# A hybrid decoder layer on one core: pinning the products of the DeltaNet systems' recursion behind the last evicted projection

## The chip, the cores and the metric

The kernel runs on one core of a Trainium2 chip. The core has a matrix engine, TensorE (PE in the rows; its weight loads are PEld), and three engines for the rest: VectorE (DVE), ScalarE (ACT) and GpSimd (POOL). SyncE (SP) issues the DMAs. Each engine works through its own list of instructions, and semaphores tie the lists together. The metric is the device time of one execution in microseconds (us), the median of several runs; the profile is of one further execution.

## The reference

One decoder layer over 1040 tokens (16 learned ones, then 1024), 1024 channels, all in float32: half a SwiGLU feed-forward block, a mixer, a second half block, a norm. The mixer holds two branches of 8 heads of 128: gated DeltaNet and retention. The DeltaNet branch is where the change lies. Cut to it:

```python
def gdn_chunk_scan(q, k, v, g, beta, state, chunk):
    ...
    a = jnp.where(strict, jnp.einsum("bhncd,bhnmd->bhncm", k_beta, k) * decay, 0.0) + jnp.eye(chunk, dtype=q.dtype)
    solve = functools.partial(lax.linalg.triangular_solve, left_side=True, lower=True)
    u = solve(a, v * beta[..., None])
    w = solve(a, k_beta * jnp.exp(g)[..., None])
    ...
    def step(s, xs):
        qk_c, u_c, w_c, qd_c, kd_c, gl_c = xs
        v_new = u_c - jnp.einsum("bhck,bhkv->bhcv", w_c, s)
        o = jnp.einsum("bhck,bhkv->bhcv", qd_c, s) + jnp.einsum("bhcm,bhmv->bhcv", qk_c, v_new)
        s = s * jnp.exp(gl_c)[..., None, None] + jnp.einsum("bhck,bhcv->bhkv", kd_c, v_new)
        return s, o
```

For each head and each chunk of tokens a unit lower triangular system `a` is solved, and then a scan carries a 128x128 state from chunk to chunk.

## The kernel before, in words

Every float32 matmul of the projections is made of three passes (L158 to L160) over numbers split in a high and a low part: ACT makes the high part of a weight tile (`wh`, L136), POOL or DVE the low part (`wl`, L137). The weights come in tiles `wraw` by DMA. The projections of the mixer are made in pairs by seven products of half blocks instead of eight (`project`), for which DVE forms sums and differences of raw weight tiles (L708, L709, L711, L712). A product ends in a bank of PSUM with the tag `mm`, of which there are two; it is evicted by a copy on ACT (L667, L705, L715, L717) or by an addition on DVE (`add`, L649). The next product but one needs the bank again.

The DeltaNet mixer is woven from four generators that each give a step at a time. `bulk` is the filling work: for each head the projection of keys and values (`kv`), a pair of gate projections, the projection of queries and of the output gate. Three others lead beside it, each at a rate of its own in steps per filling step: `all_scans` 0.6, `all_systems` 0.95, `all_queries` 0.53. `idle(n)` lets n steps of a generator pass with nothing in them. The program so traced is then put in order, engine by engine, when it is built: the builder keeps the dependencies and follows its own estimate of when each operand is there. `tc.issue_after(x)` adds one more condition to the instructions of its block: those on x's engine stand behind x in that engine's list.

`gdn_systems` prepares one head: silu and a short convolution of the keys (`cb`, L1021, L1023, L1026), the products of the keys with themselves (L1122), scaled into `X` (L1126); their 16x16 diagonal blocks (`x16`, L1131, L1132) are written to HBM and read back, repeated for each row of a block, as `xr` (two DMAs, L1144), because the recursion that inverts the blocks needs them so. The recursion is 15 times a product (`pr`, L1160) and an update of `u` by it (L1161), all on DVE, strictly one after the other; all 15 products read `xr`. Behind it PE takes `u` (L1171), and a chain of small matmuls (L1180 to L1240) between DVE and ACT turns the 16x16 inverses into the 128x128 inverse `Ut`. `gdn_scan` of a head then carries the state: in each chunk PE makes two products that read the state (L1300, L1302), two copies on ACT follow (`vn`, L1304, L1305), PE makes the update (L1308), and DVE adds it (`st`, L1310), for which the next chunk waits. Scan steps of one head lie beside the system of the next.

The pool `raw` holds the projections that are convolved or become gates, three buffers of 128x1043; `Ut` has one buffer.

Of the kernel before, what the change touches and what calls it, by code (L numbers as in the profile page):

```python
# [10 lines left out]
F32 = mybir.dt.float32  # L11
F32R = mybir.dt.float32r
AF = mybir.ActivationFunctionType
ALU = mybir.AluOpType
PSUM = bass.MemoryType.PSUM

P = 128
# [11 lines left out]
NCH = SEQ // P  # L29
CK = NCH + 1  # L30
# [27 lines left out]
W_REC = 2  # L58
W_OUT = 3
W_DMA = 1  # L60
STEPS = 1
FAST = [[(2,), (2,)], [(2,), (2,)]]
PLAIN = [[[['mm', 'mm'], ['px', 'px']], [['gx', 'gx'], ['mm', 'px']]], [[['gx', 'gx'], ['gx', 'px']], [['mm', 'gx'], ['mm', 'px']]]]
# [33 lines left out]
def hybrid_layer(ctx, tc, a):  # L97
    nc = tc.nc
    V, S, G, PE, SP = nc.vector, nc.scalar, nc.gpsimd, nc.tensor, nc.sync
# [11 lines left out]
    def psum(kind):  # L111
        return pp.tile([P, 512], F32, name=f"ps_{part[0]}_{kind}", tag=kind, bufs=PS_BUFS[kind])
# [162 lines left out]
    def ffn(fp, hidp, hT, hn, slots, spare, second, w_in, w_out, last_blocks, last_weights, tail, first, w0=None):  # L275
# [139 lines left out]
        def output(f, e, xs, steps):  # L415
# [13 lines left out]
            for i, (wh, wl) in weights():  # L429
                chain = i in (1, 3, 5)  # L430
                for j, (d, g0) in enumerate((d, g0) for d in range(2) for g0 in range(0, 2, gn)):
                    if i in (0, 1, 3):
# [8 lines left out]
                                           op0=ALU.mult, op1=ALU.add)  # L441
                for _ in range(STEPS):
                    next(steps, None)
# [62 lines left out]
    ps = psum("px")  # L506
# [132 lines left out]
    m_ctx = ExitStack()  # L639
# [5 lines left out]

    H1, H2 = slice(0, HM), slice(HM, 2 * HM)

    def add(out, x, ps):
        V.tensor_tensor(out=out, in0=x, in1=ps, op=ALU.add)  # L649

    def product(w, i, ps=None, last=True, grow=False):
        first = ps is None
# [93 lines left out]
    def idle(n):  # L746
        for _ in range(n):
            yield
# [10 lines left out]
    def run(steps):  # L759
        while True:  # L760
            try:
                next(steps)
            except StopIteration as e:
                return e.value
# [24 lines left out]
    ps = psum("gx")  # L789
# [65 lines left out]
    def chunk0(c):  # L855
        return (0, NM) if c == 0 else (NM + (c - 1) * P, P)
# [137 lines left out]
        ret_scan(h, *row)  # L994
    r_ctx.close()

    wide = m_ctx.enter_context(tc.tile_pool(name="raw", bufs=3, side="right", reuse_waits="tile"))
    mp = m_ctx.enter_context(tc.tile_pool(name="mix", bufs=1, side="right", reuse_waits="tile"))
    bp = m_ctx.enter_context(tc.tile_pool(name="systems", bufs=2, side="right", reuse_waits="tile"))
    sp = m_ctx.enter_context(tc.tile_pool(name="scan", bufs=2, side="right", reuse_waits="tile"))  # L1000
# [11 lines left out]
    def silu2(raw, which, col):  # L1012
        t0 = 0 if which else NM
        o = query_tile() if which < 2 else raw
        ct = col // P
        for b0, bn in MIX3:
            s0 = max(b0, t0)
            n = b0 + bn - s0
            d = slice(s0, s0 + n)
            c = cblk(n, wide)  # L1020
            S.activation(c, raw[:, s0:s0 + n], AF.Copy, scale=cw[:, ct:ct + 1])  # L1021
            for k in range(1, TAPS):
                V.scalar_tensor_tensor(out=c, in0=raw[:, s0 + k:s0 + k + n], scalar=cw[:, 24 * k + ct:24 * k + ct + 1],  # L1023
                                       in1=c, op0=ALU.mult, op1=ALU.add)
            yield
            S.activation(o[:, d], c, AF.Silu)  # L1026
            yield
        return o
# [66 lines left out]
    def gdn_systems(h, kraw, vraw):  # L1095
# [19 lines left out]
        ps = psum("px")  # L1115
        yield PE.matmul(ps[:NM, 0:NM], lhsT=kf[:, 0:NM], rhs=kf[:, 0:NM], start=True, stop=True)
        V.scalar_tensor_tensor(out=x16[:NM, NCH], in0=ps[:NM, 0:NM], scalar=nr2b[:NM, 0:1], in1=emm[:NM, h], op0=ALU.mult, op1=ALU.mult)
        for j in range(0, NCH, 2):
            ps = psum("px")
            for i in range(2):  # L1120
                c0, n = chunk0(j + i + 1)
                ins = PE.matmul(ps[:, i * P:(i + 1) * P], lhsT=kf[:, c0:c0 + P], rhs=kf[:, c0:c0 + P], start=True, stop=True)  # L1122
            yield ins
            for i in range(2):
                c = j + i
                V.scalar_tensor_tensor(out=X[:, c], in0=ps[:, i * P:(i + 1) * P], scalar=nr2b[:, c + 1:c + 2],  # L1126
                                       in1=ems[c // 4][:, c % 4], op0=ALU.mult, op1=ALU.mult)
# [14 lines left out]
        for t, d, o in ((xr1, x_d, 0), (xr2, x2_d, hb)):  # L1142
            src = d.rearrange("(b j) c i -> b j (c i)", j=BS)[:, o:o + hb].rearrange("b j x -> b (j x)")
            SP.dma_start(t.rearrange("p j c i -> p (j c i)"), src.unsqueeze(1).broadcast_to([P // BS, BS, src.shape[1]]))  # L1144
        yield from idle(W_DMA)
        vf = yield from silu2(vraw, 2, 2048 + h * DK)
        kvm = bp.tile([P, 2, P], F32, name="kvm", tag="Ac", bufs=1)
        ps = psum("px")
# [5 lines left out]
        u = bp.tile([P, CK, BS], F32, name="u", tag="u16", bufs=2)  # L1154
        V.tensor_copy(u, delta.unsqueeze(1).broadcast_to([P, CK, BS]))
        pr = bp.tile([P, CK, BS], F32, name="pr", tag="pr", bufs=1)
        for j in range(BS - 1):
            n = BS - 1 - j
            xj = xr1[:, j, :, j + 1:] if j < hb else xr2[:, j - hb, :, j + 1 - hb:]
            V.tensor_tensor(out=pr[:, :, :n], in0=xj, in1=u[:, :, j:j + 1].broadcast_to([P, CK, n]), op=ALU.mult)  # L1160
            V.tensor_tensor(out=u[:, :, j + 1:], in0=u[:, :, j + 1:], in1=pr[:, :, :n], op=ALU.add)  # L1161
            if j % 3 == 2:
                yield from idle(W_REC)
# [3 lines left out]
                        in1=par.unsqueeze(1).unsqueeze(3).broadcast_to([P, NCH, 2, BS]), op=ALU.mult)  # L1167
        Tc = bp.tile([P, NCH, B2], F32, name="Tc", tag="Tc", bufs=1)
        V.transpose(out=Tc, in_=Uc)
        ps = psum("px")  # L1170
# [4 lines left out]
        def blocks32(lhs, rhs):  # L1175
            ps = psum("px")
            for c in range(NCH):
                for q in range(4):
                    qs = slice(B2 * q, B2 * q + B2)
                    ins = PE.matmul(ps[qs, B2 * c:B2 * c + B2], lhsT=lhs[qs, c], rhs=rhs[qs, c], start=True, stop=True,  # L1180
                                    tile_position=(B2 * q, B2 * q))
            return ps[:, :NCH * B2].rearrange("p (c x) -> p c x", x=B2), ins

        ps, ins = blocks32(xoff, Tc)
# [3 lines left out]
        ps = psum("px")  # L1188
# [3 lines left out]
        ps, ins = blocks32(Ac, Uc)  # L1192
# [1 line left out]
        V.tensor_tensor(out=Uc, in0=Uc, in1=ps, op=ALU.add)  # L1194
        Tc = bp.tile([P, NCH, B2], F32, name="Tc", tag="Tc", bufs=1)
        V.transpose(out=Tc, in_=Uc)
        Ut = bp.tile([P, NCH, P], F32, name="Ut", tag="Ut", bufs=1)
        G.memset(Ut, 0.0)
        tmp = bp.tile([P, CK * BS * BS * 3 // 4], F32, name="tmp", tag="xr", bufs=1)
        for q in range(4):  # L1200
# [4 lines left out]
        ps = psum("px")  # L1205
# [9 lines left out]
        ps = psum("px")  # L1215
# [11 lines left out]
        ps = psum("px")  # L1227
# [4 lines left out]
        ps = psum("px")  # L1232
# [5 lines left out]
        ps = psum("px")  # L1238
# [113 lines left out]
    def branch(w, ys, b0, bn):  # L1352
        ps = psum("mm")[:, :bn]
        for j in range(0, KC, 2):
            mm3(ps, [(*w[k], ys[k][0][:, b0:b0 + bn], ys[k][1][:, b0:b0 + bn]) for k in (j, j + 1)], j == 0, j == KC - 2)
            yield BR
        return ps
# [53 lines left out]
    def all_systems():  # L1411
        while 0 not in kv:
            yield
        yield from idle(N0)
        for h in range(H):
            systems[h] = (query[h], *(yield from named(f"g{h}sys", when(kv, h, lambda *x: gdn_systems(h, *x)))))
# [28 lines left out]
    for j in range(KC):  # L1445
        w = load_w(cols(a["w_branch_gdn"], j * P))
        gt_j = yrow(gates_d[O_GA][j])
        for b0, bn in R2:
            s = slice(b0, b0 + bn)
            ps = run(branch(w, ya, b0, bn))  # L1450
# [11 lines left out]
    for b0, bn in _cut([0, 512, 768, SEQ]):  # L1462
        part[0] = "branch"
        for j in range(KC):
            w = load_w(cols(a["w_out"], j * P), eng=V if j % 2 else G)
            ps = run(branch(w, ms, b0, bn))
# [85 lines left out]
```

## Time and profile before

| what | value |
|---|---|
| median of 3 runs (lowest, highest) | 3054.97 us (3052.35, 3057.59) |
| the profiled execution: its own time, its span | 3054.29 us, 3052.6 us |
| PE busy over the span | 2905.5 us (95%) |
| DVE, ACT, POOL busy over the span | 1806.9, 1333.5, 1651.6 us |
| mean granted clock of TensorE | 0.977 of full speed |

The span runs from the first to the last instruction. The granted clock is the share of TensorE's full clock that it was given; it has two levels, 1.2 and 2.4 GHz, and 0.5 in a row is the lower one. The DeltaNet mixer runs from about 1240 to 2100 us of the span, a head in some 100 us. Idle time of an engine is put down, in the rows below, to the semaphore that ended it.

### The profile page before, as it was taken

To read this page: it belongs to the slowest core of one execution; us is meant where nothing else is said; L and a number is where in the kernel's file an instruction comes from. 1 tells how busy PE (TensorE), PEld (TensorE's weight loads), DVE (VectorE), ACT (ScalarE), POOL (GpSimd) and SP (SyncE) were. 2 spreads that over 40 slices of the span, in tenths; PEclk is the share of its full clock that TensorE was granted. 3 is DMA by queue.
4 is the path that set the end of the run, shared out by engine and by line. 5 is a ranking of instruction groups with operands and counts; after the bars stand their busy time and mean duration, and the time that the engine had idled before them with its cause. 6 is when DMAs were issued, how large, how long until landed. Compare 5 with 4: busy or idle time off the path is not lost. (4 is left out here: it accounts for less than half of the span.)

```text
span 3052.6 us, 55749 instructions
## 1 busy us (share of the span) xinstructions
PE 2905.5 (95%) x21463; PEld 2754.0 (90%) x21463; DVE 1806.9 (59%) x3299; ACT 1333.5 (44%) x2797; POOL 1651.6 (54%) x1419
## 2 busy tenths in 40 slices
PE   7999998999899999989999999999998999999998
PEld 6999998999898999978998899888888999998777
DVE  8455658777755445565555554562438655557765
ACT  4333334433545544444554555463224433335332
POOL 5555556654577655543555444445526655557652
PEclk8999999999999999989999999999999999999999
DMA  3455458633221221212212221244533355457642
GB/s 104 136 171 167 157 174 274 193 95 109 59 61 52 64 66 39 73 42 66 74 53 64 63 74 49 72 149 123 187 110 115 115 161 163 160 168 251 211 125 94
DMA packets 364413, 357.19 MB, mean 117 GB/s; under 512 B 29921, under 2 KB 294370, under 8 KB 361586
## 3 DMA queue, kind: packets, MB, share of 16 engines
q1 hardware_dynamic: 364080, 353.61, 37.2%
q8 instruction: 168, 2.75, 0.4%
q14 instruction: 99, 0.81, 0.1%
q10 hardware_dynamic: 66, 0.02, 0.0%
HBM read 263.24 MB, written 90.32 MB: 116 GB/s over the span
## 5 line engine op out<-in xcount | busy, mean ns | idle before, releaser
L137 POOL TENSOR_TENSOR wl<-wraw,wh 128x512 fp32r<-128x512 f32 x806 | 1098.8, 1371 | 1043.0 <-ACT wh L136 968.8
L136 ACT CAST wh<-wraw 128x512 fp32r<-128x512 f32 x864 | 535.9, 623 | 987.6 <-issue 229.3
L223 DVE TENSOR_TENSOR wraw<-wraw 128x512 f32<-128x512 f32 x42 | 51.5, 1226 | 163.7 <-DMA wraw<-ffn_w_in 157.1
L1023 DVE SCALAR_TENSOR_TENSOR cb<-raw,cw,cb 128x344 f32<-128x344 f32 (+2 forms) x216 | 130.7, 637 | 25.7 <-ACT cb L1021 24.0
L158 PE MATMUL ps_gate_mm<-act,wh 128*128 128x344 f32 (+1 forms) x352 | 122.6, 349 | 5.8 <-DVE raw L649 3.8
L158 PE MATMUL ps_start_mm<-on,wh 128*128 128x260 f32 x392 | 111.5, 284 | 3.1 <-ACT q L339 1.6
L159 PE MATMUL ps_gate_mm<-act,wh 128*128 128x344 f32 (+1 forms) x352 | 114.3, 325 | 0.0
L160 PE MATMUL ps_gate_mm<-act,wl 128*128 128x344 f32 (+1 forms) x352 | 114.3, 325 | 0.0
L158 PE MATMUL ps_ffn_mm<-on,wh 128*128 128x256 f32 (+1 forms) x376 | 109.5, 291 | 2.0 <-ACT q L339 1.6
L160 PE MATMUL ps_start_mm<-on,wl 128*128 128x260 f32 x392 | 110.8, 283 | 0.2 <-POOL wl L137 0.2
L159 PE MATMUL ps_start_mm<-on,wh 128*128 128x260 f32 x392 | 110.9, 283 | 0.0
L160 PE MATMUL ps_ffn_mm<-on,wl 128*128 128x256 f32 (+1 forms) x376 | 109.3, 291 | 0.0
L159 PE MATMUL ps_ffn_mm<-on,wh 128*128 128x256 f32 (+1 forms) x376 | 109.2, 290 | 0.0
L158 PE MATMUL ps_start_px<-on,wh 128*128 128x260 f32 x308 | 87.4, 284 | 1.9 <-DVE sg L295 1.9
L298 DVE TENSOR_TENSOR q<-q,q 128x260 f32<-128x260 f32 (+1 forms) x84 | 69.7, 829 | 31.8 <-ACT q L339 31.8
L160 PE MATMUL ps_start_px<-on,wl 128*128 128x260 f32 x308 | 87.7, 285 | 0.0
L159 PE MATMUL ps_start_px<-on,wh 128*128 128x260 f32 x308 | 87.6, 285 | 0.0
L159 PE MATMUL ps_start_mm<-ox,wh 128*128 128x260 f32 x292 | 83.4, 286 | 3.6 <-DVE ox L137 3.6
L158 PE MATMUL ps_start_mm<-ox,wh 128*128 128x260 f32 x292 | 83.8, 288 | 1.9 <-ACT ox L136 1.5
L160 PE MATMUL ps_start_mm<-ox,wl 128*128 128x260 f32 x292 | 83.7, 287 | 1.1 <-POOL wl L137 1.1
L388 DVE TENSOR_TENSOR sums<-sums 128x512 f32<-128x512 f32 x80 | 83.8, 1067 | 0.7
L158 PE MATMUL ps_ffn_px<-on,wh 128*128 128x256 f32 (+1 forms) x284 | 83.3, 293 | 0.9 <-ACT wh L136 0.9
(1654 smaller groups left out, 10913.1 us busy)
## 6 DMA issues: line engine op xcount, KB each, us to landing
wraw<-ffn_w_in SPq DMA_DIRECT2D x176, 256.0 KB
wraw<-w_in SPq DMA_DIRECT2D x168, 256.0 KB
sums<-ffn_w_out SPq DMA_DIRECT2D x80, 256.0 KB
sums_d<-sums SPq DMA_DIRECT2D x20, 1024.0 KB
wraw<-sums_d SPq DMA_DIRECT2D x80, 256.0 KB
opnd<-opnd_d SPq DMA_DIRECT2D x35, 520.0 KB
opnd<-opnd_d SPq DMA_DIRECT2D x35, 512.0 KB
wraw<-ffn_w_out SPq DMA_DIRECT2D x68, 256.0 KB
```

What stands on the lines that cost most here:

```text
L136: S.copy(hi, raw)
L137: (eng or G).tensor_tensor(out=lo, in0=raw, in1=hi.bitcast(F32), op=ALU.subtract)
L158: PE.matmul(ps, lhsT=wh, rhs=xh, start=first and i == 0, stop=False, skip_group_check=grow)
L159: PE.matmul(ps, lhsT=wh, rhs=xl, start=False, stop=False, skip_group_check=grow)
L160: PE.matmul(ps, lhsT=wl, rhs=xh, start=False, stop=last and i == n - 1, skip_group_check=grow)
L223: V.tensor_tensor(out=ru[0], in0=ru[0], in1=ru[1], op=ALU.add)
L298: V.tensor_tensor(out=x[:, grp], in0=x[:, grp], in1=g[:, grp], op=ALU.mult)
L388: tc.keep_in_program_order(V.tensor_tensor(out=out, in0=x, in1=y, op=op))
L1023: V.scalar_tensor_tensor(out=c, in0=raw[:, s0 + k:s0 + k + n], scalar=cw[:, 24 * k + ct:24 * k + ct + 1], in1=c, op0=ALU.mult, op1=ALU.add)
```

## The change

Three edits. First, each product `pr` of the recursion is traced inside `tc.issue_after(added[0])`, where `added[0]` is the DVE addition that `add` traced last: the product may not stand ahead of that addition on DVE. Second, six empty steps (`W_XR`) are put ahead of the recursion in each head's system. Third, the pool `raw` gets a fourth buffer and `Ut` a second.

```diff
@@ constants
+W_XR = 6
@@ mixer
+    added = [None]
+
     def add(out, x, ps):
-        V.tensor_tensor(out=out, in0=x, in1=ps, op=ALU.add)
+        added[0] = V.tensor_tensor(out=out, in0=x, in1=ps, op=ALU.add).ins
...
-    wide = m_ctx.enter_context(tc.tile_pool(name="raw", bufs=3, side="right", reuse_waits="tile"))
+    wide = m_ctx.enter_context(tc.tile_pool(name="raw", bufs=4, side="right", reuse_waits="tile"))
@@ gdn_systems
         pr = bp.tile([P, CK, BS], F32, name="pr", tag="pr", bufs=1)
+        yield from idle(W_XR)
         for j in range(BS - 1):
             n = BS - 1 - j
             xj = xr1[:, j, :, j + 1:] if j < hb else xr2[:, j - hb, :, j + 1 - hb:]
-            V.tensor_tensor(out=pr[:, :, :n], in0=xj, in1=u[:, :, j:j + 1].broadcast_to([P, CK, n]), op=ALU.mult)
+            with tc.issue_after(added[0]):
+                V.tensor_tensor(out=pr[:, :, :n], in0=xj, in1=u[:, :, j:j + 1].broadcast_to([P, CK, n]), op=ALU.mult)
             V.tensor_tensor(out=u[:, :, j + 1:], in0=u[:, :, j + 1:], in1=pr[:, :, :n], op=ALU.add)
             if j % 3 == 2:
                 yield from idle(W_REC)
...
-        Ut = bp.tile([P, NCH, P], F32, name="Ut", tag="Ut", bufs=1)
+        Ut = bp.tile([P, NCH, P], F32, name="Ut", tag="Ut", bufs=2)
```

In the changed program the lines of `gdn_systems` up to the recursion have numbers higher by 3, those behind the product by 5: the product is L1165, the update L1166, the scan's `st` L1315, the addition of a projection L652, the matmul that takes `u` L1176.

The order of instructions moves from the first head's convolutions to the end of the DeltaNet mixer; ahead of it and behind it the lists are the same. DVE's list around the first product of head 6, before (a row is line, operation, out<-in, shape of the output; `st` belongs to the scan of head 5, `raw` to an evicted gate projection):

```order
L1132 SCALAR_TENSOR_TENSOR x_21220<-Xc,masks,x_21220 128x128
L649 TENSOR_TENSOR raw<-raw,ps_gate_mm 128x344
L1317 TENSOR_TENSOR vt<-ps_g5scan_rx,vt 128x512
L649 TENSOR_TENSOR raw<-raw,ps_gate_mm 128x344
L1160 TENSOR_TENSOR pr<-xr,u 128x9x15
L1161 TENSOR_TENSOR u<-u,pr 128x9x15
L1310 SCALAR_TENSOR_TENSOR st<-st,elast,ps_g5scan_gx 128x128
L1160 TENSOR_TENSOR pr<-xr,u 128x9x14
```

The same place now:

```order
L652 TENSOR_TENSOR raw<-raw,ps_gate_mm 128x344
L711 TENSOR_TENSOR wraw<-wraw 128x512
L712 TENSOR_TENSOR wraw<-wraw 128x512
L714 TENSOR_TENSOR wraw<-wraw 128x512
L1315 SCALAR_TENSOR_TENSOR st<-st,elast,ps_g5scan_gx 128x128
L715 TENSOR_TENSOR wraw<-wraw 128x512
L652 TENSOR_TENSOR raw<-raw,ps_g6proj_mm 128x344
L1165 TENSOR_TENSOR pr<-xr,u 128x9x15
L1166 TENSOR_TENSOR u<-u,pr 128x9x15
L1165 TENSOR_TENSOR pr<-xr,u 128x9x14
```

Four weight sums, one addition to the scan's state and one more evicted projection now stand ahead of the first product. In heads 1, 2 and 5, too, the first product moves behind the addition of the projection that comes next.

DVE's list at the first product of head 4, before (`st` belongs to the scan of head 3):

```order
L1310 SCALAR_TENSOR_TENSOR st<-st,elast,ps_g3scan_gx 128x128
L649 TENSOR_TENSOR raw<-raw,ps_gate_mm 128x344
L1317 TENSOR_TENSOR vt<-ps_g3scan_rx,vt 128x512
L1160 TENSOR_TENSOR pr<-xr,u 128x9x15
L1161 TENSOR_TENSOR u<-u,pr 128x9x15
L649 TENSOR_TENSOR raw<-raw,ps_gate_mm 128x344
L1160 TENSOR_TENSOR pr<-xr,u 128x9x14
L1310 SCALAR_TENSOR_TENSOR st<-st,elast,ps_g3scan_gx 128x128
```

And now:

```order
L652 TENSOR_TENSOR raw<-raw,ps_gate_mm 128x344 x2
L1315 SCALAR_TENSOR_TENSOR st<-st,elast,ps_g3scan_gx 128x128
L1322 TENSOR_TENSOR vt<-ps_g3scan_rx,vt 128x512
L711 TENSOR_TENSOR wraw<-wraw 128x512
L1165 TENSOR_TENSOR pr<-xr,u 128x9x15
L712 TENSOR_TENSOR wraw<-wraw 128x512
L1166 TENSOR_TENSOR u<-u,pr 128x9x15
L714 TENSOR_TENSOR wraw<-wraw 128x512
L1165 TENSOR_TENSOR pr<-xr,u 128x9x14
L1166 TENSOR_TENSOR u<-u,pr 128x9x14
```

Here the first product moves behind the second of the two gate additions, but not behind the next projection; the next `st` stands eight rows behind it. Heads 3 and 7 are alike, and in head 0 the product moves behind one addition that stood three rows behind it.

## Rows read from the trace of the kernel before

**Rows 1.** PE's waits, 1240 to 2120 us: waiter <- releaser: total, times, longest

```profile
PE ps_g0sys_px L1171 <- DVE u L1161: 7.0, 1, 7.0
PE ps_g5scan_gx L1300 <- DVE st L1310: 5.6, 1, 5.6
PE ps_g1proj_mm L158 <- ACT zs L667: 4.2, 1, 4.2
PE ps_gate_mm L158 <- DVE raw L649: 3.8, 1, 3.8
PE ps_g2scan_gx L1300 <- DVE st L1310: 3.3, 2, 2.2
PE ps_g6scan_gx L1300 <- DVE st L1310: 2.3, 2, 2.0
PE ps_g4scan_gx L1300 <- DVE st L1310: 2.2, 1, 2.2
...
PE ps_g1proj_mm L158 <- DVE raw L649: 1.6, 1, 1.6
PE ps_g1scan_gx L1300 <- DVE st L1310: 1.5, 1, 1.5
PE ps_g2proj_mm L158 <- ACT raw L667: 1.3, 1, 1.3
```

**Rows 2.** DVE's waits over the same stretch

```profile
DVE pr L1160 <- DMA xr<-x_d: 37.7, 8, 7.7
```

**Rows 3.** Timeline of DVE, head 6: start, duration, instruction, idle time before it

```profile
1904.30 0.51 DVE L649 TENSOR_TENSOR raw<-raw,ps_gate_mm 128x344 f32<-128x344 f32 x1 [1.59 <-PE ps_gate_mm L160]
1912.47 0.30 DVE L1160 TENSOR_TENSOR pr<-xr,u 128x135 f32<-128x135 f32 x1 [7.65 <-DMA xr<-x_d]
...
1913.02 0.34 DVE L1310 SCALAR_TENSOR_TENSOR st<-st,elast,ps_g5scan_gx 128x128 f32<-128x128 f32 x1
```

**Rows 4.** Three stretches, PE only: length, busy (instructions), granted clock, DMA share, GB/s

```profile
1362.15:1375.80 13.65, 13.65 (x94) 0.50 0.06 14
1614.74:1618.15 3.41, 3.41 (x14) 0.50 0.00 0
1911.70:1918.53 6.83, 5.12 (x19) 0.50 0.30 110
```

**Rows 5.** Timeline of PE, head 1, then head 6: projection matmuls of 352 columns

```profile
1410.18 0.32 PE L158 MATMUL ps_g1proj_mm<-act,wh 128*128 128x352 f32 x1
...
1410.66 0.32 PE L158 MATMUL ps_g1proj_mm<-act,wh 128*128 128x352 f32 x1
...
1915.02 0.49 PE L160 MATMUL ps_g6proj_mm<-act,wl 128*128 128x352 f32 x1
...
1915.90 0.49 PE L160 MATMUL ps_g6proj_mm<-act,wl 128*128 128x352 f32 x1
```

**Rows 6.** Timeline, head 3: PE's last products of keys, DVE's first product

```profile
1593.51 0.61 PE L1122 MATMUL ps_g3sys_px<-sil 128*128 128x128 f32 x4
...
1606.06 0.30 DVE L1160 TENSOR_TENSOR pr<-xr,u 128x135 f32<-128x135 f32 x1 [3.09 <-DMA xr<-x_d]
```

**Rows 7.** Timeline of DVE, head 1: first product, a convolution step, last update

```profile
1415.38 0.30 DVE L1160 TENSOR_TENSOR pr<-xr,u 128x135 f32<-128x135 f32 x1 [6.77 <-DMA xr<-x_d]
...
1416.93 0.55 DVE L1023 SCALAR_TENSOR_TENSOR cb<-raw,cw,cb 128x328 f32<-128x328 f32 x1
...
1426.63 0.18 DVE L1161 TENSOR_TENSOR u<-u,pr 128x9 f32<-128x9 f32 x1
```

**Rows 8.** Timeline of DVE, head 0: first product, a slow update, last update

```profile
1328.12 0.30 DVE L1160 TENSOR_TENSOR pr<-xr,u 128x135 f32<-128x135 f32 x1 [3.38 <-DMA xr<-x_d]
...
1332.08 1.37 DVE L1161 TENSOR_TENSOR u<-u,pr 128x108 f32<-128x108 f32 x1
...
1346.28 0.97 DVE L1161 TENSOR_TENSOR u<-u,pr 128x9 f32<-128x9 f32 x1
```

**Rows 9.** Timeline of POOL, head 0

```profile
1332.02 3.82 POOL L137 TENSOR_TENSOR wl<-wraw,wh 128x512 fp32r<-128x512 f32 x3 [1.82 <-ACT wh L136]
```

## Prediction

> **What bounds the kernel now.** I read the views in this order: the waits of PE over the DeltaNet mixer, the waits of DVE there, timelines at the places that these named, and the granted clock behind each wait. PE is the engine that sets the end: nearly all of its work is one long list, and what it loses in the mixer it loses by single waits. The reader is to see in [rows 1] that the long ones end on DVE, or on ACT copies, and in [rows 2] that DVE itself waited 37.7 us in eight pieces, one for each head, for the same thing: the transfer `xr` that the first product of the recursion needs.
>
> [Rows 3] tie the two together. In head 6 DVE was done with a gate addition at 1904.8 us and then stood before the product for 7.65 us. Two rows behind the product stood `st`, the state of head 5's scan, and PE waited 5.6 us for it [rows 1]. DVE works in the order of its list, so what stands behind the product waits for the transfer too. Three kinds of PE's waits come of it: for `st` in five scans (5.6, 3.3, 2.3, 2.2, 1.5), for a projection's addition behind the product (3.8 and 1.6, both L649), and for an ACT copy that stands behind a silu whose convolution DVE held up (4.2 and 1.3, both L667) [rows 1]. Together 25.8 us.
>
> A long wait has a second price. Behind four of these waits the granted clock fell to 0.5, the lower of its two levels, twice for 3.4 us and twice for 6.8 us; one of each is shown [rows 4]. At the full clock three projection matmuls start within 0.48 us (0.16 each), at the lower one within 0.88 us (0.29 each) [rows 5]: 45% of such a stretch is lost. The four stretches, 20.5 us, cost 9.2 us. The product's wait for its transfer thus costs PE about 35 us in all.
>
> Head 0 is a case of its own: PE waited 7.0 us at L1171 for the end of the recursion [rows 1], and behind it lie two stretches at 0.5, one of 6.8 us and the one of 13.65 us [rows 4]: another 9.2 us.
>
> **The change, part by part.**
>
> *Fourth `raw` buffer, second `Ut` buffer.* They issue nothing. They take away reuse waits, and no wait in [rows 1] names one. I cost them at nothing; below, a gain is not excluded, since they let the later recursion of one head overlap the scan of the other, but it shows only as order, which is counted next. If `Ut` still had one buffer, its clearing would wait for the previous head's scan, and the chain behind the recursion with it.
>
> *Six steps and the pin.* They add no arithmetic either. No matmul and no transfer moves against the last key product (L1122) of its head, except that what follows the recursion comes later. I counted in the lists of both programs how many projection matmuls PE has between that key product and the projection whose addition stands last before the first product. Before: 0, 48, 30, 48, 18, 30, 30, 48 for heads 0 to 7. Now: 60, 96, 90, 36, 30, 90, 90, 36. The transfer lands about 12 us behind the key product: 1594.1 to 1606.1 us in head 3 [rows 6], and somewhat later in heads 1 and 6, where DVE waited longest for it [rows 3, 7].
>
> Heads 1, 2, 5, 6: 90 to 96 projection matmuls and 9 to 14 others at no more than 0.16 us [rows 5] are 16 to 17.5 us. The data is there before the product's turn. The waits 4.2, 1.3, 1.5, 2.2 and 5.6 (scans 1, 4, 5 lie beside heads 2, 5, 6) and two long stretches at half clock go.
>
> Heads 3, 4, 7: the pin lies only 30 to 36 matmuls behind, 6 to 7 us. DVE will still wait here, by about as much as before. But what stood close behind the product has moved: the next `st` is now eight or nine rows behind it, and the matmul that reads this `st` stands 84 to 96 projection matmuls behind the key product, with some 20 others, at about 17 us. DVE is free at 12 us and needs about 4 us for nine rows (0.3 to 0.55 us each, [rows 3, 7]), so `st` comes at 16. The waits 3.3, 3.8 and 2.0 go with their two short stretches, with a margin of only a microsecond. Head 0: the addition for which PE waited 1.6 us is now ahead of the product. So I take all of the 35 us, and for the bounds none of it in heads 0, 3, 4, 7 (1.6, 3.3, 3.8, 2.0 and 3.1 for clock, 13.8 us).
>
> *What is late next: the end of the recursion.* Behind it PE's list holds L1176, and behind that projections, none of which can pass it. PE now meets it 144 to 174 projection matmuls behind the key product, 92 to 120 before. In head 1, 79 matmuls lie between the pinned projection and L1176: 12.6 us at 0.16. The recursion of head 1 took 11.4 us with five other rows among its thirty [rows 7]; now 15 others stand there, ten more at about 0.55 us, a convolution step's time [rows 7], so 16.9 us. PE waits 4.3 us that it did not wait before, and by the pattern of [rows 4] a stretch of 6.8 us at half clock follows, 3.1 us. Cost 7.4, bounds 0 and 12. In heads 2, 5, 6, 80 to 93 matmuls (12.8 to 14.9 us) face a recursion with four to six other rows (11 to 12 us): covered by 2 to 3 us. In heads 3, 4, 7 the recursion starts at 12 us and holds 11 or 12 other rows, so it ends at 26.6 to 27.3; PE comes at 177 to 183 matmuls, 28.3 to 29.3 us. Covered by 2 us.
>
> Head 0: the recursion took 19.1 us with ten other rows [rows 8], now 19, so 24 us from the landing at 13: 37, against L1176 at 201 matmuls or 32 us. The wait would be 5 instead of 7. But much of the 19.1 is slow instructions: an update took 1.37 us [rows 8] while POOL split weights [rows 9], where a product takes about 0.3 us [rows 3]. Without such meetings it ends in time. Bounds: nothing gained, or 7.0 and the 9.2 of clock, 16. I take 3.5, half of the wait, since the slow rows are as likely in the new place.
>
> The order of every list in the mixer is new, and the waits not shown in [rows 1] will fall elsewhere. I add 5 us, two new waits like the 2.2 of [rows 1]; bounds 0 and two such waits with a short stretch each, 8.
>
> **The sum.** -35 - 3.5 + 7.4 + 5 = -26. The profiled execution took 3054.3 us, 0.7 us less than the median of the runs: 3028 in its terms, 3029 for the median.
>
> **A rule against it.** An update of the recursion takes 0.3 us alone and 1.37 us beside POOL's splits [rows 8, 9]. The Trainium skill (GPSIMD Engine Reference, 1. Specifications) says that GpSimd's SBUF interfaces are shared with VectorE and contended by VectorE instructions with two SBUF inputs; every product and every update here is one, and the trace agrees at this place. By that rule, moving the recursion into POOL's busy time lengthens it, and the sum would turn into that of the slower rival below.
>
> **The rivals.**
> The pin binds too early. In heads 0, 3, 4, 7 the product still waits, and what is behind it is still late. For it: the counts 60, 36, 30, 36 against a landing at 12 us. Against: the `st` rows moved back. The gain is then 21.2 instead of 35, head 0 gives nothing: -21.2 + 7.4 + 5 = -9, 3046.
>
> The end of the recursion takes the place of the transfer: besides head 1, three or four of the heads with 2 us of cover wait at L1176 like head 1, 7.4 each. For it: head 0 did so before. Against: the counts above. -26 + 3.5 x 7.4 = 0: about 3055, no change.
>
> Slower: the recursion meets POOL's work in every head as in head 0. Head 0's 19.1 us exceed head 1's 11.4 [rows 7, 8] by 7.7, of which five more rows explain 2.8; 5 us are left. A recursion that ends 5 us later than planned, less 1 to 2 us of cover, keeps PE 3.5 us at L1176 and brings 3.1 of clock: 6.6 in each of eight heads, 53 us. The change loses from 4.4 us a head (35 over 8), which is 1.3 us of wait if each brings a long stretch at half clock. -35 + 53 + 5 = +23: 3078. Against: POOL splits weights beside every head, and head 1 still took 11.4 us [rows 7].
>
> Better than forecast: no wait in head 1, and head 0's whole wait and clock gone: -35 - 16 + 3 = -48, 3007.
>
> **How the numbers follow.** Chances: forecast (3014 to 3042) 0.58, too early 0.17, better 0.07, no change 0.08, slower 0.10. 0.2% of the median is 6.1 us, about what a measurement of this kernel tells from no change. Faster by more: 0.58, 0.07 and nine tenths of 0.17, 0.80; same 0.09; slower 0.11. The predicted time is the likeliest case's, 3029. The range for 8 in 10 goes from 3007, the better case, to 3052, which takes in the early pin and its spread, and leaves out the slower case and most of no change.
>
> **What would show it.** DVE's total wait for `xr` falls from 37.7 us to some 10 to 15, all of it in heads 0, 3, 4, 7, and none in 1, 2, 5, 6. PE's waits for `st` in the scans fall from 15 us to under 3, and the two waits for ACT copies at L667 in heads 1 and 2 are gone, and with them the half-clock stretches at these places. A new wait at L1176 in head 1 of about 4 us, and one in head 0 of 3 to 4. The prediction is wrong if L1176 waits in more than three heads, if `st` still waits in heads 3, 4, 7, or if new waits stand where none of these rows is, in the chain behind the recursion (L1180 to L1240 before) or at the gates.

## The result, and the profile after

The changed kernel took 3094.4 us (median of 4 runs, 3089.99 to 3099.85), the kernel before, run beside it, 3053.7 us. The ratio is 1.0137, 95% interval 1.0118 to 1.0155: slower by 1.4%, where the prediction said 3029 us and gave slower a chance of 0.11. The profiled execution took 3099.85 us with a span of 3098.0, 45.4 us longer than that of before.

First the waits of PE over the mixer, 1240 to 2120 us, in the columns of [rows 1]:

```profile
PE ps_g0sys_px L1176 <- DVE u L1166: 9.1, 1, 9.1
PE ps_g4sys_px L1214 <- DVE Tc L1201: 4.0, 1, 4.0
PE ps_g6proj_mm L159 <- DVE raw L652: 3.5, 1, 3.5
PE ps_g6sys_px L1214 <- DVE Tc L1201: 3.2, 1, 3.2
PE ps_g2proj_mm L159 <- DVE raw L652: 2.9, 1, 2.9
...
PE ps_g7sys_px L1214 <- DVE Tc L1201: 2.5, 1, 2.5
PE ps_g7sys_px L1224 <- DVE tmp L1219: 2.5, 1, 2.5
PE ps_g5sys_px L1214 <- DVE Tc L1201: 2.4, 1, 2.4
PE ps_g3sys_px L1214 <- DVE Tc L1201: 1.7, 1, 1.7
PE ps_g2sys_px L1176 <- DVE u L1166: 1.7, 1, 1.7
PE ps_g4sys_px L1176 <- DVE u L1166: 1.6, 1, 1.6
```

No scan waits for `st` any more, and no projection for the copies at L670 (L667 before) by more than 0.3 us. Of DVE's waits there is left, against [rows 2]:

```profile
DVE pr L1165 <- DMA xr<-x_d: 11.9, 4, 3.8
```

So the old waits went. In their place stands a column of waits that [rows 1] does not have: at L1214, in heads 3 to 7. That is the third block of the chain behind the recursion, in which small matmuls of 32x32 and 64x64 turn the 16x16 inverses into `Ut`; it waits for DVE's transpose `Tc`. All of PE's waits over 0.4 us in the mixer come to 44.3 us before and 45.0 after: what was taken away came back elsewhere, and in waiting the change is neutral.

The loss is in the clock. PE at four stretches of the changed kernel, in the columns of [rows 4]; the first lies in head 0, the others in heads 3, 4 and 5:

```profile
1349.00:1359.24 10.24, 3.77 (x73) 0.50 0.00 0
1645.94:1669.83 23.89, 22.60 (x133) 0.50 0.03 12
1755.17:1775.65 20.48, 19.56 (x139) 0.50 0.04 14
1864.40:1884.88 20.48, 20.48 (x140) 0.50 0.04 14
```

Before, the mixer had 54.6 us at half clock in eight stretches, the longest 13.65 us; now it has 157.0 us in thirteen, seven of them over 13 us. PE is busy almost throughout a long one, so no view of waits or busy shares shows it; the row of granted clock does. 45% of a stretch is lost, by the starts in [rows 5]: over the whole span 103.1 us more at half clock and 1.6 us more waiting make 48.0 us, against 45.4 measured.

How a long stretch begins, in head 4. DVE's timeline:

```profile
1748.87 0.42 DVE L1192 COPY Ac<-ps_g4sys_px 128x256 f32<-128x256 f32 x1 [1.64 <-PE ps_g4sys_px L1194]
1749.21 0.69 DVE L711 TENSOR_TENSOR wraw<-wraw 128x512 f32<-128x512 f32 x1
1749.93 1.41 DVE L712 TENSOR_TENSOR wraw<-wraw 128x512 f32<-128x512 f32 x1
1751.37 1.66 DVE L714 TENSOR_TENSOR wraw<-wraw 128x512 f32<-128x512 f32 x1
1752.96 0.41 DVE L1199 TENSOR_TENSOR Uc<-Uc,ps_g4sys_px 128x256 f32<-128x256 f32 x1
1753.29 2.30 DVE L1026 SCALAR_TENSOR_TENSOR cb<-raw,cw,cb 128x344 f32<-128x344 f32 x2
1755.51 0.43 DVE L1201 STREAM_TRANSPOSE Tc<-Uc 128x256 f32<-128x256 f32 x1
```

And PE's:

```profile
1751.81 0.32 PE L161 MATMUL ps_g5proj_mm<-act,wl 128*128 128x352 f32 x1
1756.09 1.70 PE L1214 MATMUL ps_g4sys_px<-Tc,X 32*32 32x32 f32 x32 [3.97 <-DVE Tc L1201]
1757.72 0.66 PE L159 MATMUL ps_g5proj_mm<-act,wh 128*128 128x352 f32 x1
...
1759.78 1.73 PE L1224 MATMUL ps_g4sys_px<-Uc,tmp 32*32 32x32 f32 x32
```

Between the copy `Ac` and the transpose `Tc` DVE's own part of the chain is one row, L1199. Now three sums of the next pair's weights (L711, L712, L714, some of them slowed to 1.4 and 1.7 us) and two convolution steps (L1026) stand there, and `Tc` is late. From the end of `Ac` to the end of `Tc` it is 6.65 us, against 3.64 in head 4 before, where L1194 stood alone there. Of heads 3 to 7, three had no foreign row at this place before and two had one; now each has three to five (sums of weights in heads 3 to 5, convolution steps in 3 to 6, weight splits on DVE in 7). PE has six projection matmuls between two blocks of the chain, waits 3.97 us, and 0.9 us before the wait ends the clock falls to half. There it stays until 1775.65 us, 1.5 us before the end of the chain's last matmul. Two of the seven long stretches have another start: 13.65 us in head 1 lie behind a wait of 2.7 us in a scan (L1304, for `Qk`), and 17.07 us in head 2 behind one of 1.1 us at L1224.

### The profile page after: what moved, and what is told of

It reads as the page before. It is cut to its first block, busy times and chain, and to the rows that moved or that the text cites. A ratio compares the mean times of both kernels' runs of the same rounds, so it can differ in the third digit from the quotient of the medians.

```text
span 3098.0 us, 55744 instructions
## 1 busy us (share of the span) xinstructions
PE 2949.1 (95%) x21463; PEld 2796.3 (90%) x21463; DVE 1825.4 (59%) x3299; ACT 1334.5 (43%) x2797; POOL 1661.4 (54%) x1419
## 5 line engine op out<-in xcount | busy, mean ns | idle before, releaser
L1026 DVE SCALAR_TENSOR_TENSOR cb<-raw,cw,cb 128x344 f32<-128x344 f32 (+2 forms) x216 | 145.5, 703 | 14.6 <-ACT cb L1024 13.4
L161 PE MATMUL ps_ffn_px<-on,wl 128*128 128x256 f32 (+1 forms) x284 | 83.2, 293 | 0.8 <-POOL wl L138 0.8
```

Source lines behind the costliest of these rows:

```text
L161: PE.matmul(ps, lhsT=wl, rhs=xh, start=False, stop=last and i == n - 1, skip_group_check=grow)
```

## The experiments

All in us, from the profiled executions: PE's waits of over 0.4 us and the time at half clock in the mixer (1240 to 2120 us; before 44.3 and 54.6), then the differences from the kernel before over the whole span. "Priced" is the difference of waits plus 0.45 of that of half clock.

| run | ratio [95%] | waits, mixer | half clock, mixer | waits | priced | span |
|---|---|---|---|---|---|---|
| changed kernel | 1.0137 [1.0118, 1.0155] | 45.0 | 157.0 | +1.6 | +48.0 | +45.4 |
| bufs_only | 0.9992 [0.9977, 1.0007] | 40.3 | 64.9 | -8.4 | -10.1 | -7.9 |
| pin_only | 0.9960 [0.9946, 0.9974] | 41.3 | 51.2 | -5.3 | -11.5 | -8.2 |
| pin_bufs | 0.9945 [0.9925, 0.9965] | 42.2 | 41.0 | -4.4 | -10.6 | -14.3 |
| six_bufs | 1.0172 [1.0148, 1.0197] | 56.5 | 139.9 | +12.8 | +49.7 | +51.6 |
| pin_six | 1.0114 [1.0093, 1.0135] | 48.4 | 146.8 | +3.6 | +42.3 | +37.7 |
| xr3 | 1.0006 [0.9992, 1.0019] | 39.7 | 78.5 | -7.2 | +3.8 | +1.9 |
| xr12 | 1.0076 [1.0061, 1.0091] | 51.5 | 71.7 | +11.0 | +19.0 | +21.2 |
| relief | 1.0030 [1.0011, 1.0049] | 39.9 | 61.4 | -3.5 | -1.0 | +2.3 |
| fill | 1.0077 [1.0056, 1.0099] | 35.7 | 95.6 | -13.4 | +4.7 | +21.5 |
| delay | 0.9993 [0.9976, 1.0010] | 42.8 | 54.6 | -6.3 | -3.2 | -2.3 |
| delay2 | 1.0174 [1.0141, 1.0207] | 64.7 | 126.3 | +17.7 | +46.8 | +40.9 |
| delay_dense | 1.0168 [1.0145, 1.0192] | 70.4 | 88.7 | +21.0 | +34.4 | +49.2 |

Priced and span agree within 6 us wherever PE has no work added. fill and delay_dense add 120 matmuls each, 19 us at the 0.16 us of [rows 5]; with them 24 and 54 stand against 21.5 and 49.2. A row is one execution, so its span need not say what the ratio of the medians says: bufs_only has -7.9 us beside 0.9992. Outside the mixer, time at half clock lies between 74 and 95 us in these executions.

**Which part costs.** Four runs with one part of the change left out, or alone.

bufs_only, from the changed kernel:

```diff
-        yield from idle(W_XR)
-            with tc.issue_after(added[0]):
-                V.tensor_tensor(out=pr[:, :, :n], ...
+            V.tensor_tensor(out=pr[:, :, :n], ...
```

> Only the fourth raw buffer and the second Ut buffer; no pin, no empty steps. The changed kernel loses about 41 us, and by its trace all of it is time at the lower clock (157 us in the mixer instead of 55), not waiting (46 us instead of 47). Theory S (the six empty steps put the chain of small matmuls behind the recursion into DVE's weight sums of the next pair): 3054 within 6 us, half-clock time in the mixer about 55 us, eight waits for xr. Theory P (the pin stretches the recursion): the same, 3054 within 6. Theory B (the buffers let other work move in front of the chain): 3075 to 3095, half-clock time above 100 us.

pin_bufs, from the changed kernel:

```diff
-        yield from idle(W_XR)
```

> The full change without the six empty steps. Theory S: the loss goes, and some of what the pin should give comes: 3030 to 3050, waits of PE for Tc at L1213 under 3 us in all, half-clock time at most 60 us. Theory P: the loss stays, 3080 to 3095, recursions of 14 to 28 us. Theory B: the loss stays.

six_bufs, from the changed kernel:

```diff
-            with tc.issue_after(added[0]):
-                V.tensor_tensor(out=pr[:, :, :n], ...
+            V.tensor_tensor(out=pr[:, :, :n], ...
```

> The full change without the pin. Theory S: the loss stays, 3080 to 3100, PE waits for Tc in most heads, half-clock time above 120 us; DVE waits little for xr, since six steps alone move the recursion. Theory P: 3030 to 3050. Theory B: the loss stays.

pin_six, from the changed kernel:

```diff
-tile_pool(name="raw", bufs=4, ...
+tile_pool(name="raw", bufs=3, ...
-name="Ut", tag="Ut", bufs=2)
+name="Ut", tag="Ut", bufs=1)
```

> The full change without the buffers (raw three, Ut one). Theories S and P: still slower than before by 30 us or more, 3085 to 3105, perhaps more, since the clearing of the one Ut then waits for the scan before. Theory B: 3030 to 3055.

The kernels with the six steps lose, with or without the pin or the buffers; those without them don't. Of the three theories that is S, and pin_bufs at 3040.3 us is faster than both kernels of this study. six_bufs, at 3107.2 us, is slower than S had it, and DVE's wait for `xr`, expected to be small there, stayed (38.7 us). In six_bufs, without the pin, the wait for `Tc` stands in PE's list too, and the stretch beside it is 17.07 us long:

```profile
PE ps_g6sys_px L1213 <- DVE Tc L1200: 4.3, 1, 4.3
```

The pin alone gains: pin_only, the kernel before with the pin and nothing else, was expected at 3035 to 3045 us if the buffers do nothing, and took 3044.2; bufs_only can't be told from the kernel before. But the gain is not by what the prediction gave as its reason. In pin_bufs the waits of DVE for the transfer and of PE for `st` are still there; first DVE's row, then one of PE's:

```profile
DVE pr L1164 <- DMA xr<-x_d: 30.5, 8, 7.2
```

```profile
PE ps_g5scan_gx L1304 <- DVE st L1314: 5.1, 1, 5.1
```

To take those away, both steps and pin were needed (37.7 us before, 11.9 with both, 16.0 in pin_six, 38.7 in six_bufs). What pin_bufs saves in the mixer is 2.1 us of waiting and 13.6 us at half clock, all of the latter in head 0, where the two stretches of 6.83 and 13.65 us became one of 6.83: PE's wait for `Tc` there, 2.1 us before, is 0.8.

**How it goes with the number of steps.**

```diff
-W_XR = 6
+W_XR = 3
```

> The changed kernel with 3 empty steps ahead of the first product instead of 6. Theory S (the loss is the place of the small-matmul chain: with six steps DVE's Tc stands behind the next pair's weight sums L711 to L714 and convolutions, TensorE waits 1.7 to 4.0 us for it at the matmuls of L1214 in heads 3 to 7, and each wait opens a half-clock stretch of 14 to 24 us): the chain moves back by some 18 projection matmuls, about 3 us, so some heads come out ahead of the weight sums and others not; half-clock time in the mixer between the 41 us of no steps and the 157 us of six, 60 to 110 us, and 3050 to 3075 us. Theory P (the steps cost in proportion, since each lets foreign work into the recursion on DVE): half of the 54 us between no steps (3040) and six (3094), 3067 us. The two differ little here; the run is the near point of a series with 12 steps.

```diff
-W_XR = 6
+W_XR = 12
```

> The changed kernel with 12 empty steps instead of 6. Theory S: the chain moves on by some 36 projection matmuls, about 6 us, and a part of the heads is then past the weight sums: half-clock time not above the 157 us of six steps by more than 20, 3060 to 3105 us. Theory P (cost in proportion to the steps, 9 us a step): 3040 + 12 x 9 = 3148 us.

3054.4 and 3077.3 us: with no steps 0.9945, with three 1.0006, with six 1.0137, with twelve 1.0076. More steps are not dearer as such, so theory P, here a cost in proportion to the steps, falls; and the recursions, first product to last update, are longest with twelve (203 us over the eight heads, 147 with six, 116 before), so their length isn't the price either. With twelve, long half-clock stretches are left in heads 1, 5 and 7 alone. Its largest wait is a new one, for a convolution in the last head, which no theory had foreseen:

```profile
PE ps_g7q_gx L1074 <- ACT cb L1070: 10.2, 1, 10.2
```

**Taking the wait away from the changed kernel.** relief puts projections ahead of the block, fill puts work that does nothing there.

```diff
+        yield from idle(3)
         At = tmp[:, :512].rearrange("p (c x) -> p c x", x=64)
         ps = psum("px")
```

> The changed kernel with three empty steps more, but these ahead of the matmuls of L1214, behind DVE's transpose Tc: some 18 projection matmuls (2.9 us at full clock) stand there before TensorE comes to wait for Tc. Theory S with the wait as the start of the half-clock stretches: the waits of 1.7 to 4.0 us at L1214 in heads 3 to 7 fall to under 1.1 us, the stretches of 14 to 24 us that follow them go in three to five heads, half-clock time falls from 157 us to 60 to 100, and the time to 3050 to 3075 us. Rival C (the chain's 32x32 and 64x64 matmuls run at half clock by themselves wherever they lie this close to the weight sums, whether or not TensorE waited): waits fall but the stretches stay, 3085 to 3100 us. Theory P (steps as such cost): three more steps, 3094 to 3120 us.

```diff
         At = tmp[:, :512].rearrange("p (c x) -> p c x", x=64)
         ps = psum("px")
+        if h >= 3:
+            for i in range(24):
+                PE.matmul(ps[:, :HM], lhsT=ops[0][0][:, 0, :P], rhs=ops[0][0][:, i % 4], start=True, stop=True)
```

> The changed kernel with work added: in heads 3 to 7, 24 matmuls of 128x128 by 128x344 whose results are overwritten stand just ahead of the matmuls of L1214, in the place where TensorE waits 1.7, 4.0, 2.5, 3.2 and 2.5 us for Tc (13.9 us in all). At 0.16 us each they take 3.8 us per head, 19 us in all. Theory S with the wait as the start: the waits become work, the stretches of 23.9, 20.5, 20.5, 13.7 and 17.1 us at half clock (95.6 us) go or shrink to one of 3.4 to 6.8 us each; at 45 per cent of a stretch lost, that gives back 28 to 43 us against 5 us of added work: 3055 to 3072 us, though the kernel does more. Rival C (the chain runs at half clock by itself): the stretches stay and the matmuls cost at least 19 - 13.9 = 5 us: 3095 to 3110 us. Theory that the waiting alone is the loss: 3095 to 3100 us, since the added work fills the wait and shortens nothing.

relief: 3060.3 us, 34 us less than the changed kernel, with three steps more. The longest wait at this block is 0.5 us now (head 3), and half-clock time is 61.4 us, as expected; what stays of the long stretches are 13.65 us each in heads 3 and 4 and 10.2 in heads 0 and 7. The one in head 4 starts at a wait of 2.5 us for a convolution (L1074); the one in head 3 has no wait over 0.5 us in the 20 us before it.

fill: 3079.1 us, 15 us less, though PE does 20 us more; expected were 22 to 39 less. Three stretches, in heads 3, 4 and 5:

```profile
1650.78:1654.19 3.41, 3.41 (x18) 0.50 0.21 77
1756.59:1773.66 17.07, 17.07 (x83) 0.50 0.04 16
1865.82:1869.23 3.41, 3.41 (x22) 0.50 0.21 77
```

PE's timeline in head 3 shows the added block at full clock and no wait behind it:

```profile
1640.48 3.96 PE L1213 MATMUL ps_g3sys_px<-act 128*128 128x344 f32 x24
1644.37 1.09 PE L1217 MATMUL ps_g3sys_px<-Tc,X 32*32 32x32 f32 x32
```

In heads 3, 5, 6 and 7 the stretches of 23.9, 20.5, 13.7 and 17.1 us became 3.4, 3.4, none and 10.2, and heads 0 to 2, which were not touched, kept theirs. In head 4 a stretch of 17.1 us came all the same, 6.8 us further on in the chain, with no wait over 0.7 us in the 20 us before it: a wait there is enough for a long stretch, as the next runs show, but it isn't the only way into one. That is the part of rival C that holds, and at 45% it is 7.7 us, about what fill missed its range by. What starts this stretch, and that of head 3 in relief, stays open.

**Putting the wait into a kernel that has none at this place.** From pin_bufs, six additions on DVE; in the second form held in place.

```diff
         V.tensor_tensor(out=Uc, in0=Uc, in1=ps, op=ALU.add)
+        if h >= 3:
+            for i in range(6):
+                V.tensor_tensor(out=xr[:, :512], in0=xr[:, 512:1024], in1=xr[:, :512], op=ALU.add)
         Tc = bp.tile([P, NCH, B2], F32, name="Tc", tag="Tc", bufs=1)
         V.transpose(out=Tc, in_=Uc)
```

> The pin and the buffers without the six steps (3040 us, no wait over 1 us at the matmuls of L1214 in heads 3 to 7 and no half-clock stretch over 3.4 us there), with work added on DVE: in heads 3 to 7, six additions of 128x512 on a row that is no longer read stand between the sum Uc and the transpose Tc. At 0.70 us each, Tc comes 4.2 us later and TensorE waits some 3.5 us for it, about the wait of head 4 in the changed kernel, with everything else in its old place. Theory S with the wait as the start: each wait opens a half-clock stretch that lasts through the chain's small matmuls, 10 to 20 us, 50 to 100 us more at half clock, so 17 us of waiting and 22 to 45 us of clock: 3079 to 3102 us. The waits alone (the half-clock stretches of the changed kernel belong to its other order, not to a wait): 5 x 3.5 = 17 us, 3055 to 3062 us. DVE's work hidden after all: 3040 to 3045 us.

delay tells nothing of the question: the builder put the additions, for which nothing waits, ahead of the chain (the first at 1605.2 us, beside head 3's recursion), and `Tc` came when it had come before. The 30 additions, 20 us of DVE, cost 0.5% against pin_bufs.

```diff
-        V.tensor_tensor(out=Uc, in0=Uc, in1=ps, op=ALU.add)
+        last = V.tensor_tensor(out=Uc, in0=Uc, in1=ps, op=ALU.add).ins
+        if h >= 3:
+            for i in range(6):
+                with tc.issue_after(last):
+                    last = V.tensor_tensor(out=xr[:, :512], in0=xr[:, 512:1024], in1=xr[:, :512], op=ALU.add).ins
         Tc = bp.tile([P, NCH, B2], F32, name="Tc", tag="Tc", bufs=1)
-        V.transpose(out=Tc, in_=Uc)
+        with tc.issue_after(last):
+            V.transpose(out=Tc, in_=Uc)
```

> The run before (delay) with its additions in the place where they were meant to stand: in heads 3 to 7, six additions of 128x512 pinned between DVE's sum Uc and its transpose Tc; there they stood, unpinned, ahead of the chain. The kernel is otherwise that with the pin and the buffers and no steps (3040 us; TensorE comes to the matmuls behind Tc about 0.6 us after Tc is there in head 4). At 0.68 us each (the first run's trace) Tc comes 4.1 us later, so TensorE waits some 3.5 us a head, 17 us in all. Theory S with the wait as the start: each wait opens a half-clock stretch of 10 to 20 us that lasts through the chain's small matmuls; 17 us of waiting and 22 to 45 us of clock: 3079 to 3102 us. The waits alone, each with a stretch of 3.4 to 6.8 us as the waits of the kernel before have (a loss of 1.5 to 3 us each): 17 + 8 to 15 = 25 to 32 us, 3065 to 3072 us; waits that open no stretch at all: 3057 us.

3104.8 us, 2.3% above pin_bufs: more than the loss of the changed kernel, from one delay in five heads. In heads 4, 5 and 7 the long stretch lies beside PE's wait for `Tc` (5.9, 5.2 and 2.4 us); in heads 3 and 6 the longest wait beside it is one of a scan for POOL's `vt` (3.1 and 4.9 us), and `Tc` itself costs 0.9 us or nothing. PE's timeline in head 4, and the stretches of heads 4 and 5:

```profile
1736.42 0.60 PE L1094 MATMUL ps_g4scan_gx<-ident,sil 128*128 128x128 f32 x4
1742.95 1.73 PE L1218 MATMUL ps_g4sys_px<-Tc,X 32*32 32x32 f32 x32 [5.93 <-DVE Tc L1205]
```

```profile
1741.18:1761.66 20.48, 18.71 (x137) 0.50 0.00 1
1853.82:1877.71 23.89, 20.85 (x144) 0.50 0.01 1
```

The same place in pin_bufs, by the same view, where PE's longest wait is 1.2 us:

```profile
1722.00:1742.00 20.00, 18.83 (x249) 1.00 0.09 28
```

PE is as busy in the one as in the other, and got through 249 instructions where it now gets through 137. The time is a little above the range expected, because an addition took up to 1.4 us and the wait in head 4 was 5.9 us instead of 3.5.

**What keeps the clock down.** delay2 with the 24 matmuls of fill one step behind the wait, ahead of the next block:

```diff
         ps = psum("px")
+        if h >= 3:
+            for i in range(24):
+                PE.matmul(ps[:, :HM], lhsT=ops[0][0][:, 0, :P], rhs=ops[0][0][:, i % 4], start=True, stop=True)
         for e in (0, 64):
```

> The run with the pinned additions (delay2, 3105 us; in heads 3 to 7 a wait of 0.9 to 5.9 us at the matmuls behind Tc, and half-clock stretches of 10.2, 20.5, 23.9, 13.7 and 17.1 us there, 85 us) with 24 matmuls of 128x128 by 128x344 more, in heads 3 to 7, one step behind that wait, ahead of the second block of small matmuls; their results are overwritten. The wait stays as it is; what follows it is dense now. Theory K (a wait starts the half clock, and the chain's small matmuls with six projection matmuls between each two blocks keep it): the added matmuls end the stretches after some 10 us, so they come down to 3.4 to 10.3 us each, 30 to 50 us in all; added work 24 x 0.16 to 0.29 us = 4 to 7 us a head, 19 to 35 us, less 16 to 25 us of clock: 3095 to 3120 us. Rival L (the length of the wait sets the length of the stretch): the stretches stay at 85 us or grow, and the added work costs 27 to 35 us: 3130 to 3145 us.

3102.3 us, and a ratio that can't be told from that of delay2: 120 more matmuls cost nothing measurable. (Its span in the table is 8 us longer, but delay2's profiled execution was the fastest of its four.) The waits of heads 4 and 5 are the same to the hundredth (5.93 and 5.19 us), and the stretches of heads 3, 4, 5 and 6 are now those below. Head 7 has two of 6.83, so 51 us in all, just over the 30 to 50 expected, against 85.

```profile
1627.43:1637.67 10.24, 8.02 (x56) 0.50 0.08 28
1743.48:1753.72 10.24, 7.60 (x53) 0.50 0.01 2
1859.54:1866.37 6.83, 6.83 (x51) 0.50 0.00 0
1968.76:1979.00 10.24, 8.59 (x57) 0.50 0.07 27
```

In head 4 the clock came back within the added matmuls, and the next blocks of the chain run at full speed:

```profile
1749.65 5.79 PE L1227 MATMUL ps_g4sys_px<-act 128*128 128x344 f32 x24
1755.37 1.09 PE L1231 MATMUL ps_g4sys_px<-Uc,tmp 32*32 32x32 f32 x32
```

So a wait of the same length has a stretch of 20.48 us with it when the chain follows, and 10.24 when dense matmuls do; in head 5 it is 23.89 against 6.83. Rival L, by which these two would have stayed, falls. Heads 3 and 6 say less: 10.24 in both runs, and 13.65 against 10.24.

Theory K holds for the chain in heads 4 and 5, but small tiles are not the only work that the low clock lasts through. In head 1 of the changed kernel it lasted 13.65 us over projection matmuls in groups of six, with scan matmuls and blocks of one-column matmuls between them. First the stretch, then one of these blocks:

```profile
1475.28:1488.93 13.65, 13.65 (x58) 0.50 0.16 43
```

```profile
1479.31 1.28 PE L1074 MATMUL ps_g2sys_px<-ones,cb 128*128 128x1 f32 x6
```

What such work has in common with the chain, no run here shows.

## Why the prediction was wrong

*The transfer's 35 us: right as a mechanism.* DVE's wait for `xr` fell to 11.9 us, all of it in heads 0, 3, 4 and 7, as forecast; the waits for `st` and at L670 went, in heads 3, 4 and 7 too, where the margin was called a microsecond. As a gain the 35 us were seen in no run: relief, with no wait over 0.5 us at L1214, stands at 1.0030, with 39.9 us of other waits in the mixer.

*Head 0, -3.5: the wait wrong in sign, the sum about right.* The wait at L1176 is 9.1 us instead of 7.0; the recursion took 28.0 us, where 24 were reckoned. Behind it came one stretch of 10.2 us instead of 6.8 and 13.65, which gives back 4.6, so that wait and clock together come to -2.5, near the forecast by luck.

*Head 1, +7.4: in another place.* There is no wait at L1176. The recursion was longer than the 16.9 us reckoned (19.6), but PE had been held up on its way: an addition of the next projection (L652) stands among the recursion's last rows, and PE waited 2.9 us for it, with 3.4 us at half clock behind. That is 4.4 us. Heads 2 and 4 waited 1.7 and 1.6 us at L1176.

*The step that failed* is "What is late next: the end of the recursion", together with "I add 5 us, two new waits like the 2.2". It followed PE's list to L1176, called the rest covered, and stopped. The next things on that list are the chain's blocks with six projection matmuls between each two, each waiting for DVE; and six steps move that chain into the time in which DVE has the next pair's sums and convolutions to do. The order of DVE's list for head 4 stood in the section on the change with L711, L712 and L714 among the products; nobody asked what stands among the rows after the products. L1214 and L1224 waited 19.2 us in all, and additions at L652 10.3 us, against the 4.4 allowed. New waits in this chain were one of the prediction's own signs of being wrong, but no rival and no term of the sum gave them a price.

*The larger error is the price of a wait.* It was taken as 3.4 to 6.8 us at half clock, from waits for `st` and for projections, behind which dense projections follow. [Rows 4] held the other case, 13.65 us inside head 0's chain, and it was set down to that head's wait of 7.0 us at L1171, which had ended some 15 us earlier. PE's list of waits before has another, which ended 0.7 us ahead of that stretch, at the block that is L1214 now:

```profile
PE ps_g0sys_px L1209 <- DVE Tc L1196: 2.1, 1, 2.1
```

So the long price at this very place was on record. By delay2 and delay_dense it goes with what follows the wait. From 1620 us on, where heads 3 to 7 lie, half-clock time rose from 23.9 to 105.8 us, 82 of the 102 us by which it grew in the mixer; at 45% that is 37 us, more than the 35 that the change was to save.

*The rivals.* "Slower" had the right sign by another way: it saw the loss in slow updates beside POOL. Those did grow, from 25.5 to 31.6 us over all heads (each product or update over its median, where over by more than 0.25 us), but 6 us in eight heads are not 53, and with recursions of 203 us xr12 lost half as much as the changed kernel. Where POOL did cost something is in the chain: beside the sums of 1.41 and 1.66 us in head 4, which take 0.69 in head 2, and the convolution steps behind them, 1.02 and 1.36 us where 0.57 is the median, POOL's timeline has

```profile
1749.44 1.35 POOL L1332 TENSOR_TENSOR vt<-vt,sc 128x512 f32<-128x512 f32 x1
1750.76 1.72 POOL L138 TENSOR_TENSOR wl<-wraw,wh 128x512 fp32r<-128x512 f32 x1
1752.45 1.49 POOL L1269 TENSOR_TENSOR kte<-kt,eg 128x512 f32<-128x512 f32 x1
1754.01 1.20 POOL L1271 TENSOR_TENSOR kt<-kt,kd_s 128x512 f32<-128x512 f32 x1
```

Those four rows ran 2.9 us over their medians, ahead of a `Tc` for which PE waited 3.97 us. In heads 3 to 7 together, the rows that now stand between `Ac` and `Tc` ran 8.1 us over, each slow one beside work of POOL, against 13.9 us of waiting at L1214. So the rival was right that DVE loses time beside POOL, and wrong on where: not in the recursion but in the chain, where the six steps put those rows. What would be left of the loss without it, no run shows.

*The clock.* The waits and 0.45 of the time at half clock make 48.0 us, against 45.4 measured. The Trainium skill (TensorE: Matmul & The Clock Gate, HAM oscillation — how this bites in real kernels) describes a kernel whose matrix engine falls to the lower clock at each of its waits, and counts half of the time at that clock as lost, beside the waits themselves. The traces agree that it is a price of its own; they put it at 45%, and by the page's half it would be an estimated 53 us. That the time until the clock is back depends on what follows the wait is from the runs here.

## What to carry to other kernels

Before a step is moved, follow everything behind it to the end of its chain, and for each matmul of the chain ask what stands in the other engine's list ahead of its operand at the new place; here only the first, L1176, was checked, and L1214 took the gain. Price a wait of the matrix engine by what follows it: in this kernel it cost, beside its own length, mostly 1.5 to 3 us in front of dense matmuls (stretches of 3.4 to 6.8), and mostly 6 to 11 in front of small-tile matmuls (13.7 to 23.9). And change one thing at a time: the pin alone, with or without the buffers, gains 0.4 to 0.55%, and the six steps beside it turned that into a loss of 1.4%.

## What the runs showed of the hardware that was not expected

PE can be busy for all of a stretch and still stay at the lower clock: 20.48 us busy of 20.48 at 0.50 in head 5, with blocks of 32x32 and 64x64 matmuls, six projection matmuls between each two, and a few other matmuls. Head 4's chain ran through at 1.00 in pin_bufs, where the longest wait in the 20 us ahead of it was 1.2 us (18.83 us busy of 20.00), and nearly all of it at 0.50 in delay2, where it was 5.9. So either level can hold over the same mix of work. In heads 4 and 5 of delay2 the wait decided which, and filling it took the long stretch away in three of fill's five heads; two long stretches, in fill and in relief, began without such a wait. And work that is thrown away can be free: 120 matmuls made fill 15 us faster than the kernel that they were added to, and cost delay_dense nothing that can be told from noise.
